# The last head of a chunked Delta net layer: its k and q projected ahead of v and z, one more head's output product inside the output pieces, and the residual added by VectorE

## The chip, the cores and the metric

One NeuronCore of a Trainium2 chip runs the whole program. The metric is the device time of one execution in microseconds (us), the median of several runs. The engines are TensorE (PE; its weight loads are listed as PEld), VectorE (DVE), ScalarE (ACT), GpSimd (POOL) and SyncE (SP), which issues most transfers.

## The reference

Two encoder layers act on 512 tokens of width 1024, each followed by a squared-ReLU MLP. The first mixer is a bidirectional gated Delta net with 8 heads of 128 keys and 128 values, in chunks of 64; the second is a gated linear attention (GLA). Cut to the Delta net and to what surrounds it:

```python
proj = h @ w_in                                  # q, k, v, z of 8 heads, gates
qkv  = silu(depthwise_conv5(proj[..., :3072]))
q, k = l2norm(q) * 128 ** -0.5, l2norm(k)
o    = delta(q, k, v, beta[0], g[0]) + flip(delta(flip(q), flip(k), flip(v), ...))
o    = rmsnorm(o, norm_g) * silu(z)
m    = o @ w_out                                 # (512, 1024) @ (1024, 1024)
x    = layernorm(alpha * x + m)                  # alpha = 4 ** 0.25
x    = layernorm(alpha * x + relu(x @ w1) ** 2 @ w2)
```

## The kernel before, in words

Numbers are float32. A product of two float32 matrices is made of three products of their rounded parts (`mm3`, lines 114 to 116): high by high, high by low, low by high. `split` (lines 95 and 96) makes the parts, the high one by a cast on ACT, the low one by a subtraction on DVE.

The Delta net layer (`gdn`) runs over its heads in a staggered loop of 10 steps. Step i traces the recurrence of head i-2 (`recur`), the solve of head i-1 (`solve`, the inverse of the chunk's triangular matrix), the projections of head i (`project`) and its row factors (`rows`), and at the end `finish` of head i-2, which norms, gates and splits that head's output into its high and low parts. Below, solve(7) means the solve of head 7, which is the last one. In steps 8 and 9 no head is left to project; there the output pieces run, `out_pieces`: the product of heads 0 to 5 with one half (512 columns) of w_out in each step, whose result is added to alpha times x (line 252) and kept in the tiles z.

The order in which an engine gets its instructions is fixed before the run by a planner. It goes by its own estimate of times, and takes among the instructions whose inputs and buffers are then at hand the one traced first. So what is traced later (projections, output pieces) stands between the small steps of what is traced earlier (recurrence, solve). Each engine then takes its instructions strictly in that order, and waits where an input is late.

The names that the steps touch:

- `project` (line 1264 is the SiLU): for one head four projections, in the order k, q, v, z, 24 matmuls each into a PSUM bank with the tag "pj" (three banks). k, q and v go through a convolution of five taps (line 1230 on ACT, line 1234 on DVE). For head 0 SiLU of k and q is called as soon as q is there; for the other heads one call after z does all four. Each call is followed by a load of the table set for exp and ln (line 55).
- `rows`: transposes k and q (PSUM tag "tp", one bank), sums their squares on ACT (line 1286), and ends in the row factors rt (line 1309).
- `solve`: needs rt in `ep` (line 1342), which takes both PSUM banks of the tag "ac"; the same banks are used by all its steps. It ends with xf (line 1483).
- `recur`: lines 1511 to 1536, four steps in both directions; it ends with the output product op (line 1544).
- `finish`: squares (line 1556), scaling (1562), transposes (1566), gate (1572, tile p), and the two parts oh (1573) and ol (1576).
- `out_last`: the product of heads 6 and 7 with both halves of w_out, for four tiles of 128 tokens, followed by LayerNorm of each tile and its transposition for the MLP (lines 159 to 163). In the Delta net it starts each PSUM bank with a float32 product of z with the identity (line 271), and LayerNorm reads the banks. In the GLA layer it is called with `in_ps=False`: there the residual is added by DVE (line 277), which leaves the row sums, and the squares are summed on ACT (line 204).
- `layernorm`: mean and variance by `bn_stats` (lines 208, 209), or from given sums (lines 202 to 205); then lines 211 to 219.

The weights of out_last go into buffers of their own (`homes`): those of the first half into the pair "oah"/"oal", those of the second into two of the four tiles "ol", which hold the low parts of heads 0 to 7, two heads to a tile.

## Time and profile before

| what | value |
|---|---|
| time, median of 3 runs | 1383.04 us (1381.99 to 1383.33) |
| profiled execution, span from the first to the last instruction | 1383.4 us |
| mean granted TensorE clock | 0.996 |
| head 7: last projection done, end of `finish` | 341.6 us, 420.4 us |
| first matmul of the MLP behind it | 435.0 us |

The profiled execution has no time of its own beside its span; the span lies 0.4 us above the median of the runs. In the rows of the profile a line such as `L1342 PE MATMUL ep<-rt,sel` names the line of the program, the engine, the operation, and the tiles written and read. In a timeline the first two numbers are the start and the duration in us, and what stands in square brackets is the idle time before and what ended it. In grouped rows the number after x is a count, then come the sum in us and the mean in ns. Matmuls overlap, so a duration of 0.39 us does not mean that one starts every 0.39 us; 0.23 us is the distance between two starts of the form 128x512.

### The profile page before, as it was taken

To read this page: it belongs to the slowest core of one execution; us is meant where nothing else is said; L and a number is where in the kernel's file an instruction comes from. 1 tells how busy PE (TensorE), PEld (TensorE's weight loads), DVE (VectorE), ACT (ScalarE), POOL (GpSimd) and SP (SyncE) were. 2 spreads that over 40 slices of the span, in tenths; PEclk is the share of its full clock that TensorE was granted. 3 is DMA by queue.
4 is the path that set the end of the run, shared out by engine and by line. 5 is a ranking of instruction groups with operands and counts; after the bars stand their busy time and mean duration, and the time that the engine had idled before them with its cause. 6 is when DMAs were issued, how large, how long until landed. Compare 5 with 4: busy or idle time off the path is not lost.

```text
span 1383.4 us, 21226 instructions
## 1 busy us (share of the span) xinstructions
PE 1353.9 (98%) x8361; PEld 1130.9 (82%) x8361; DVE 1073.9 (78%) x1682; ACT 736.6 (53%) x1438; POOL 71.8 (5%) x111
## 2 busy tenths in 40 slices
PE   9999999999999999999999999999999999999997
PEld 8777787777777888888887888888878888888876
DVE  6687787778677997887957587866879787979665
ACT  4676568665743655555543354654446455546440
POOL 4000000000003600000000000000000000000000
PEclk9999999999999999999999999999999999999999
DMA  6221112211251523253132322221225153431141
GB/s 177 74 62 47 46 32 62 52 42 32 79 154 56 172 77 109 74 153 92 47 112 75 96 89 62 61 62 61 87 66 177 52 152 92 122 88 50 46 151 47
DMA packets 146122, 117.11 MB, mean 85 GB/s; under 512 B 7632, under 2 KB 122440, under 8 KB 146024
## 3 DMA queue, kind: packets, MB, share of 16 engines
q1 hardware_dynamic: 144679, 111.57, 27.4%
q0 software_dynamic: 1344, 4.20, 1.1%
q8 instruction: 65, 1.06, 0.3%
q14 instruction: 34, 0.27, 0.1%
HBM read 113.66 MB, written 2.10 MB: 84 GB/s over the span
## 4 chain that ended last, share of the span: by engine, by line
PE 86%; ACT 6%; DVE 5%; DMA 2%; issue 1%; POOL 0%; DVEq 0%; ACTq 0%; POOLq 0%
PE pj L115 5%; PE pj L116 5%; PE pj L114 5%; PE pjv L114 3%; PE pjv L115 3%; PE pX L114 3%; PE pjv L116 3%; PE pX L115 3%; PE pX L116 3%; PE scp L851 2%; PE fxz L114 2%; PE op L1544 2%; PE fxz L115 2%; PE fxz L116 2%; DMA wst<-in_mlp_w 2%; PE pl L115 2%
## 5 line engine op out<-in xcount | busy, mean ns | idle before, releaser
L95 ACT CAST wh<-wst 128x1024 fp32r<-128x1024 f32 x146 | 152.9, 1050 | 221.6 <-PE pj L115 50.7
L96 DVE TENSOR_TENSOR wl<-wst,wh 128x1024 fp32r<-128x1024 f32 x146 | 177.8, 1225 | 73.3 <-ACT wh L95 73.1
L115 PE MATMUL pj<-xtl,wh 128*128 128x512 f32 (+1 forms) x352 | 127.9, 363 | 0.5 <-DVE xtl L163 0.5
L114 PE MATMUL pj<-xth,wh 128*128 128x512 f32 (+1 forms) x352 | 127.4, 363 | 0.8 <-ACT xth L162 0.7
L116 PE MATMUL pj<-xth,wl 128*128 128x512 f32 (+1 forms) x352 | 127.4, 362 | 0.0
L96 DVE TENSOR_TENSOR w2l<-w2r,w2h 128x1024 fp32r<-128x1024 f32 x84 | 102.5, 1223 | 26.3 <-ACT w2h L95 26.3
L95 ACT CAST w2h<-w2r 128x1024 fp32r<-128x1024 f32 x84 | 88.2, 1050 | 63.5 <-PE pX L116 28.1
L115 PEld LDWEIGHTS pj<-xtl,wh 128*128 128x128 f32 x352 | 67.2, 191 | 10.9 <-DVE xtl L163 0.8
L114 PEld LDWEIGHTS pj<-xth,wh 128*128 128x128 f32 x352 | 66.9, 191 | 11.2 <-ACT xth L162 1.2
L116 PEld LDWEIGHTS pj<-xth,wl 128*128 128x128 f32 x352 | 67.1, 191 | 10.2
L115 PE MATMUL pX<-w2l,ah 128*128 128x512 f32 x192 | 75.0, 391 | 0.0
L116 PE MATMUL pX<-w2h,al 128*128 128x512 f32 x192 | 74.9, 390 | 0.0
L114 PE MATMUL pX<-w2h,ah 128*128 128x512 f32 x192 | 74.8, 393 | 0.0
L95 ACT CAST ah<-h 128x1024 fp32r<-128x1024 f32 x46 | 48.4, 1053 | 47.1 <-PE pX L115 19.3
L336 DVE TENSOR_TENSOR w2r<-w2r 128x1024 f32<-128x1024 f32 x48 | 57.5, 1222 | 0.3
L96 DVE TENSOR_TENSOR al<-h,ah 128x1024 fp32r<-128x1024 f32 x46 | 56.3, 1223 | 0.6
L114 PE MATMUL pjv<-wh,xth 128*128 128x512 f32 x128 | 54.8, 428 | 0.0
L116 PE MATMUL pjv<-wh,xtl 128*128 128x512 f32 x128 | 50.2, 392 | 0.0
L115 PE MATMUL pjv<-wl,xth 128*128 128x512 f32 x128 | 50.0, 390 | 0.0
L116 PEld LDWEIGHTS pX<-w2h,al 128*128 128x128 f32 x192 | 36.1, 188 | 7.5
L116 PE MATMUL pjk<-xth,wl 128*128 128x512 f32 (+1 forms) x112 | 41.8, 373 | 0.0
L114 PE MATMUL pjk<-xth,wh 128*128 128x512 f32 (+1 forms) x112 | 41.7, 372 | 0.0
(477 smaller groups left out, 3932.0 us busy)
## 6 DMA issues: line engine op xcount, KB each, us to landing
wst<-in_mlp_w SPq DMA_DIRECT2D x80, 512.0 KB, 4.4
w2r<-in_mlp_w SPq DMA_DIRECT2D x48, 512.0 KB, 3.8
wst<-in_a_w_in SPq DMA_DIRECT2D x32, 512.0 KB, 4.1
wst<-in_b_w_in SPq DMA_DIRECT2D x32, 256.0 KB, 3.0
wst<-in_a_w_out SPq DMA_DIRECT2D x8, 512.0 KB, 3.7
wst<-in_b_w_in SPq DMA_DIRECT2D x8, 512.0 KB, 3.8
wst<-in_b_w_out SPq DMA_DIRECT2D x8, 512.0 KB, 3.5
xt<-in_x SPq DMA_DIRECT2D x4, 512.0 KB, 5.3
```

The costliest lines, as they stand in the source:

```text
L95: nc.scalar.copy(hi, src)
L96: nc.vector.tensor_tensor(lo, src, hi.bitcast(F32), ALU.subtract)
L114: mm(ps, ah, bh, start=start, stop=False, **kw)
L115: mm(ps, ah, bl, start=False, stop=False, **kw)
L116: mm(ps, al, bh, start=False, stop=stop, **kw)
L336: V.tensor_tensor(blocks[a + (q,)], blocks[a + (q,)], blocks[b + (q,)], ALU.add)
L851: T.matmul(ps[:, n, :], kh[:, sl], qh[:, sl], start=True, stop=True)
L1544: T.matmul(op[:, n, :], l, r, start=i == 0, stop=i == len(mm) - 1)
```

## The change

Three things are changed, nearly all at the end of the Delta net layer.

1. The last head projects like head 0: SiLU of k and q is called after q, and `rows` is traced after q, ahead of v and z. v and z get a SiLU call of their own after z. Head 0, which has the two calls already, now gets the new place of `rows` as well; since its `project` yields once and not eight times for k, the sixteen steps reach into v, and `rows` is traced after 21 of the 24 products of v.
2. The output pieces of the second half take in head 6 as well. The block of weights of heads 6 and 7 for that half is loaded there, into "oah"/"oal", and kept (`held`) for out_last, which then has heads 6 and 7 to do in the first half and head 7 alone in the second. The weights of the first half go into the tiles "ol".
3. The option `in_ps` goes away: the Delta net's out_last adds the residual on DVE with row sums, as the GLA layer does already.

```diff
-    def out_pieces(self, w, ks, lhs, z, tag, halves=(0, 1), piece=2):
+    def out_pieces(self, w, ks, lhs, z, tag, halves=(0, 1), piece=2, keep=None):
         for hf in halves:
-            ws = [self.wrows(w, k * P, hf * 512) for k in ks[::2]]
+            ws = [self.wrows(w, k * P, hf * 512, keep[1] if keep and k + 2 > ks[-1] else None) for k in ks[::2]]
+            if keep:
+                keep[0][hf] = {ks[::2][-1]: ws[-1]}
...
-    def out_last(self, w, ks, lhs, z, tags, par, homes=None, xtags=("tp",), ahead=None, in_ps=True):
+    def out_last(self, w, ks, lhs, z, tags, par, homes=None, xtags=("tp",), ahead=None, held=()):
...
-        ws = [{k: self.wrows(w, k * P, hf * 512, next(homes, None)) for k in ks[hf][::2]} for hf in range(2)]
+        ws = [held[hf] if hf in held else {k: self.wrows(w, k * P, hf * 512, next(homes, None)) for k in ks[hf][::2]}
+              for hf in range(2)]
...
-            if in_ps:
-                nc.tensor.matmul(ps, self.ident, z[t][hf], start=True, stop=False)
             for i, k in enumerate(ks[hf]):
                 ah, al = lhs(k, sl)
-                wh, wl = ws[hf][k - i % 2]
-                self.mm3(ps, ah, al, wh[:, i % 2, :], wl[:, i % 2, :], not in_ps and i == 0, i == len(ks[hf]) - 1)
-            if not in_ps:
-                nc.vector.scalar_tensor_tensor(z[t][hf], ps, 1.0, z[t][hf], ALU.mult, ALU.add, accum_out=sums[t][:, hf:hf + 1])
+                wh, wl = ws[hf][k - k % 2]
+                self.mm3(ps, ah, al, wh[:, k % 2, :], wl[:, k % 2, :], i == 0, i == len(ks[hf]) - 1)
+            nc.vector.scalar_tensor_tensor(z[t][hf], ps, 1.0, z[t][hf], ALU.mult, ALU.add, accum_out=sums[t][:, hf:hf + 1])
             if hf:
                 banks, last = [pss[t, 0], pss[t, 1]], t == NT - 1
-                if in_ps:
-                    self.layernorm(banks, self.xh(t), par, last)
-                else:
-                    self.layernorm(z[t], self.xh(t), par, last, None if last else (sums[t], banks))
+                self.layernorm(z[t], self.xh(t), par, last, None if last else (sums[t], banks))
...
             if new:
-                run(new.project(done), new.rows(done))
-            if i >= A_H:
-                load_z(i - A_H)
-                run(c.out_pieces(w_out, early, lhs, z, "pj", (i - A_H,), 1))
+                work = new.project(done)
+                if new.first_kq:
+                    for _ in range(2 * KT):
+                        next(work)
+                    run(new.rows(done))
+                    run(work)
+                else:
+                    run(work, new.rows(done))
+            if i == A_H:
+                load_z(0)
+                run(c.out_pieces(w_out, early, lhs, z, "pj", (0,), 1))
+            if i == A_H + 1:
+                load_z(1)
+                run(c.out_pieces(w_out, early + [6], lhs, z, "pj", (1,), 1, (held, (pool, "oah", "oal", 1))))
...
-        c.out_last(w_out, [[6, 7]] * 2, lhs, z, ("pj", "ac"), par,
-                   [(pool, "oah", "oal", 1), (pool, "ol", "ol", NT)], ahead=lambda: c.take_ahead(w_next, 3))
+        c.out_last(w_out, [[6, 7], [7]], lhs, z, ("pj", "ac"), par, [(pool, "ol", "ol", NT)],
+                   ahead=lambda: c.take_ahead(w_next, 3), held=held)
...
+        self.first_kq = h in (0, A_H - 1)
...
-            if i == 1 and h == 0:
+            if i == 1 and self.first_kq:
                 c.exp_ln_after(A.activation(kq, kq, AF.Silu))
                 done.add(("kq", h))
             elif i == 3:
-                v = sil[:, 2 if h == 0 else 0:4, :]
+                v = sil[:, 2 if self.first_kq else 0:4, :]
```

More of the change, by code (lines that the diff above doesn't have):

```diff
@@ L254, in out_pieces @@
                         yield 0.68 * piece, 0.0
-    def out_last(self, w, ks, lhs, z, tags, par, homes=None, xtags=("tp",), ahead=None, in_ps=True):
+    def out_last(self, w, ks, lhs, z, tags, par, homes=None, xtags=("tp",), ahead=None, held=()):
         nc = self.nc
         homes = iter(homes or ())
-        ws = [{k: self.wrows(w, k * P, hf * 512, next(homes, None)) for k in ks[hf][::2]} for hf in range(2)]
+        ws = [held[hf] if hf in held else {k: self.wrows(w, k * P, hf * 512, next(homes, None)) for k in ks[hf][::2]}
+              for hf in range(2)]
         if ahead:
             ahead()
-        sums = [None if in_ps else self.small.tile([P, 2], F32, name="lns", tag="lns") for t in range(NT)]
+        sums = [self.small.tile([P, 2], F32, name="lns", tag="lns") for t in range(NT)]
         pss = {}
@@ L742, in gla @@
                    [(pool, "oah", "oal", 1), (pool, "v", "sr", 2), (pool, "F", "F", 2), (pool, "v", "sr", 2)],
-                   ahead=lambda: c.take_ahead(w_next, 3), in_ps=False)
+                   ahead=lambda: c.take_ahead(w_next, 3))
 class GlaHead:
@@ L1183, in run @@
                     pass
-        done = set()
+        done, held = set(), {}
         for i in range(A_H + 2):
```

## The prediction

> **What bounds the kernel now.** I read the page first, for the engine that could be the limit, then the busy time in four stretches around the change, then the engines' timelines along the last head, and last the chain of waits.
>
> ```profile
> span 1383.4 us, 21226 instructions
> PE 1353.9 (98%) x8361; PEld 1130.9 (82%) x8361; DVE 1073.9 (78%) x1682; ACT 736.6 (53%) x1438; POOL 71.8 (5%) x111
> PE 86%; ACT 6%; DVE 5%; DMA 2%; issue 1%; POOL 0%; DVEq 0%; ACTq 0%; POOLq 0%
> ```
>
> TensorE is busy nearly everywhere and carries 86% of the chain. The change touches the end of the Delta net layer, and its first head. Here are four stretches of it: from the start of solve(0) to the last projection (pjz) of head 7, from there to the end of that head's `finish`, on to the first matmul of the MLP, and the first 5 us of the MLP. The columns after the length are busy us of PE, PEld, DVE, ACT and POOL, then the granted clock.
>
> ```profile
> 60.00:341.60 281.60, 276.78 (x2413) 219.35 (x2414) 222.13 (x461) 187.41 (x531) 0.00 (x0) 1.00 0.18 48
> 341.60:420.40 78.80, 78.03 (x625) 60.70 (x624) 54.54 (x116) 48.66 (x147) 2.37 (x4) 1.00 0.36 108
> 420.40:435.00 14.60, 12.74 (x54) 8.42 (x52) 13.97 (x32) 4.59 (x11) 2.99 (x2) 1.00 0.00 1
> 435.00:440.00 5.00, 4.64 (x25) 4.47 (x26) 4.86 (x15) 1.48 (x4) 1.57 (x1) 0.66 0.02 3
> ```
>
> In the second stretch PE is full, but with what? Only a chain of small steps must be done: head 7's rows, solve, recurrence, finish. The rest, the output pieces (oa), stands between them because it is at hand. In the third DVE is full (13.97 of 14.60) and PE is not: LayerNorm sets the pace there. In the fourth the clock has fallen to 0.66.
>
> [...]
>
> Now head 7's chain, by line and start, first on ACT, then DVE, then PE:
>
> ```profile
> 341.57 1.05 ACT L95 CAST wh<-wst 128x1024 fp32r<-128x1024 f32 x1 [6.41 <-PE pjz L115]
> 343.12 1.28 ACT L1264 ACT_TABLE_LOAD   x1
> 344.41 1.92 ACT L1264 ACTIVATE sil<-sil 128x2048 f32<-128x2048 f32 x1
> 346.36 1.07 ACT L1432 CAST pz<-lv 32x128 f16<-32x128 f32 x4
> 347.45 1.28 ACT L55 ACT_TABLE_LOAD   x1
> 358.59 0.57 ACT L1309 COPY rt<-rtp 6x512 bf16<-6x512 bf16 x1
> ```
>
> ```profile
> 337.07 0.74 DVE L1234 SCALAR_TENSOR_TENSOR sil<-pjq,cw,sil 128x510 f32<-128x510 f32 x1
> 355.38 1.33 DVE L1483 SCALAR_TENSOR_TENSOR xf<-Xd,nw 128x512 f32<-128x512 f16 x2
> 397.36 1.47 DVE L1483 SCALAR_TENSOR_TENSOR xf<-Xd,nw 128x512 f32<-128x512 f16 x2
> 419.61 0.82 DVE L1576 TENSOR_TENSOR ol<-p,oh 128x256 fp32r<-128x256 f32 x2
> ```
>
> ```profile
> 361.55 0.60 PE L1342 MATMUL ep<-rt,sel 6*128 6x512 bf16 x2
> 398.39 0.38 PE L1519 MATMUL m<-vt,xf 128*128 128x128 f32 x2
> 407.87 0.39 PE L116 MATMUL oa<-wh,ol 128*128 128x512 f32 x1
> 435.04 0.51 PE L114 MATMUL pj<-xth,wh 128*128 128x256 f32 x2 [0.67 <-ACT xth L162]
> ```
>
> Head 7's q is convolved by 337.8 (337.07 + 0.74), but its SiLU waits for z until 344.4. So `rows` ends with the copy of rt at 359.2, and the first step of solve(7) that needs it, ep, starts at 361.55. Solve(6) had given its last result (xf) at 356.7. From ep on everything is a chain: 36.8 us to the first recurrence product (398.39), 22.0 more to the end of finish (ol, 420.4), 14.6 more to the MLP (435.04).
>
> **The change part by part.**
>
> *k and q first.* Nothing leaves PE: two projections of 24 products move behind `rows`, and the 8 transposes and 4 row products of `rows` move ahead of them. What is added on ACT is one more SiLU call and two more table loads.
>
> ```profile
> L1264 ACT ACTIVATE sil<-sil x8: 1060/1920/1923, 48.6 to 344.4; 128x2048 f32<-128x2048 f32 x7, 128x1024 f32<-128x1024 f32 x1
> ```
>
> Head 0 already does it this way, so the form is in the trace: 1.06 us for 1024 columns. Two such calls instead of one of 1.92 add 0.2 us, and two loads of 1.28 add 2.6: 2.8 us of ACT. Where? The kq call becomes ready at 337.8, inside the 6.41 us in which ACT stood idle (335.2 to 341.57). Load, SiLU and load are 3.6 us and fit there; if that cover is gone they stand ahead of solve(6)'s casts on ACT and cost up to 3.6. The second call falls where the one of 1.92 fell and is 0.9 shorter. What ACT queues behind the new SiLU is solve(6)'s casts of pz, Dd and Xd; PE waits for those.
>
> The Trainium skill, "ScalarE: Activation LUTs", section What ACT_TABLE_LOAD costs, puts a change of table at some 2.66 us with a drain behind the load. By it the two more would cost 5.3. The trace disagrees: load at 343.12, SiLU at 344.41, 1.29 later.
>
> `rows` is then done some 5 us early (16.1 us lie between L1264's load at 343.12 and the end of rt at 359.2; from 337.8 that gives about 354). But solve(7) cannot use all of it. ep needs both PSUM banks of the tag "ac", and solve(6) gives the last one back with xf at 356.7. So ep moves from 361.55 to about 356.8: **4.8 us earlier**. Below: 0, if the planned order leaves ep where it is. Above: 5.7, if solve(6) too ends earlier, by the 0.9 of the shorter SiLU ahead of its casts (L1432). I take 4.8; the 36.8 + 22.0 us behind it keep their length, since PE's filling is the same kind of matmul as before.
>
> *Head 0 as well.* It too now has `rows` traced earlier: `project` of head 0 yields only once for k, so the sixteen steps reach 21 of the 24 products of v, and `rows` comes ahead of the last three and of z.
>
> ```profile
> 47.34 1.28 ACT L1264 ACT_TABLE_LOAD   x1
> 59.98 0.57 ACT L1309 COPY rt<-rtp 6x512 bf16<-6x512 bf16 x1 [2.53 <-PE rtp L1307]
> ```
>
> The SiLU of v and z with its two loads (47.34 to 51.0, 3.7 us) stands among the squares of `rows`; those may now go first, and rt end up to 3.7 earlier. From there to head 7 PE has projections to fill every gap (first row of the stretches, 276.78 of 281.60 busy), so I take 0. The planner deals all that follows anew, though: 1.5 either way, for the places of the identity products and of single waits move with it.
>
> *No identity products.* Eight fp32 products of z with the identity go, each two instructions. The chain of waits names three of them:
>
> ```profile
> 408.26 0.86 PE ob L271 x2
> 417.65 0.86 PE ob L271 x2
> 419.31 0.86 PE ob L271 x2
> 420.17 0.23 PE ob L114
> ```
>
> All eight are 8 x 0.86 = 6.9 us of PE, which is not what they are worth. Three stand ahead of a step of head 7: a recurrence product, the last transpose of finish, the first product with head 7. Something else at hand will take each place, a product of 0.23 at least, and the third was half covered by the wait for ol. So 2 x 0.63 plus 0.3: **1.5 us**. The five others lie where PE waits anyway. Ends: 0 and 6.9.
>
> *Residual by VectorE with sums.* The second layer's output (layer GLA) already works in this way, so each new operation has a row. First DVE and its statistics in this layer, then DVE and ACT in the other one (count | total us, mean ns):
>
> ```profile
> L208 DVE BATCH_NORM_STATS2 bst<-ob 128x6 f32<-128x512 f32 x8 | 5.5, 685 | 0.5 <-PE ob L116 0.5
> ```
>
> ```profile
> L277 DVE SCALAR_TENSOR_TENSOR xt<-ob,xt 128x512 f32<-128x512 f32 x8 | 5.5, 689 | 1.8 <-PE ob L116 1.7
> L208 DVE BATCH_NORM_STATS2 bst<-xt 128x6 f32<-128x512 f32 x2 | 1.4, 688 | 0.0
> L277 DVE DVE_READ_ACCUMULATOR xt<-ob,xt 128x1 f32 x8 | 0.7, 83 | 0.0
> L202 DVE SCALAR_TENSOR_TENSOR bmv<-lns,bias 128x1 f32<-128x1 f32 x3 | 0.7, 220 | 0.1
> L205 DVE SCALAR_TENSOR_TENSOR bmv<-lnq,bias 128x1 f32<-128x1 f32 x3 | 0.6, 214 | 0.0
> ```
>
> ```profile
> L204 ACT ACTIVATE ob<-xt,bmv 128x512 f32<-128x512 f32 x6 | 4.1, 682 | 6.2 <-DVE bmv L202 6.2
> L204 ACT ACTIVATION_READ_ACCUMULATOR ob<-xt,bmv 128x1 f32 x6 | 1.1, 188 | 0.0
> ```
>
> DVE loses six statistics (4.1) and three of four aggregations (0.6) and gains 5.5 + 0.7 + 0.7 + 0.6: 2.8 us more over four tiles. The MLP needs tiles 0 and 1 to start, and their share is 4 x 0.77 + 2 x 0.43 - 4 x 0.69 - 2 x 0.2 = 0.8. ACT gains 5.2, with room. How long it takes from the first half tile on DVE to tile 1's first transposed half on ACT can be read in both layers:
>
> ```profile
> 420.91 2.11 DVE L208 BATCH_NORM_STATS2 bst<-ob 128x6 f32<-128x512 f32 x3 [0.48 <-PE ob L116]
> ```
>
> ```profile
> 434.41 0.59 ACT L162 CAST xth<-tp 128x512 fp32r<-128x512 f32 x1 [1.16 <-PE tp L159]
> ```
>
> ```profile
> 1016.39 0.69 DVE L277 SCALAR_TENSOR_TENSOR xt<-ob,xt 128x512 f32<-128x512 f32 x1 [0.72 <-PE ob L116]
> ```
>
> ```profile
> 1030.05 0.59 ACT L162 CAST xth<-tp 128x512 fp32r<-128x512 f32 x1 [1.45 <-PE tp L159]
> ```
>
> 13.5 us here, 13.7 there, where the products came more slowly. I take **0.5 us later**, between 0.2 and 0.8.
>
> *Head 6 inside the pieces.* Twelve products of head 6 (second half) move from out_last ahead of head 7's end: 12 x 0.23 = 2.8 us of filling for places that identity products held. No DMA is added; one weight block (512 KB) is issued with the pieces instead of after them, on the same SP queue. What is new is a wait: the first half's weights for heads 6 and 7 went into a free pair of buffers, and now go into those of the low parts of heads 0 to 3, which the last output piece still reads. That piece ended at 408.3; with twelve more products, and less PE work elsewhere, I expect 411 to 413. Behind it the split needs 1.05 on ACT (L95) and some 1.2 on DVE. If it ends after head 7 does (420.4 - 4.8 - 1.5 = 414.1), tile 0 is late by up to 2.3; else 0. I take **0.5 later**.
>
> Sum: -4.8 - 1.5 + 0.5 + 0.5 = -5.3. The profiled span is 1383.4, the median of the runs 1383.04, so the execution is an ordinary one: 1383.04 - 5.3 = **1377.7 us**. The MLP behind it only shifts.
>
> **The rivals.**
>
> *PE is the limit after all.* Then all 6.9 us of identity products count, and the idle of the third stretch (14.60 - 12.74 = 1.9) is filled by the earlier chain: 1383.04 - 8.8 = 1374.2. For it: 78.03 of 78.80 busy. Against: the chain behind `ol` is DVE's.
>
> *The chain does not start earlier.* ep stays at 361.5, because the planned order, buffers or the two loads hold it. What is left is -1.5 + 0.5: 1382.0. For it: the order of each engine is fixed before the run, and ACT waited 6.41 us on a full ring while work lay ready.
>
> *The LayerNorm tail gets longer and colder: slower.* Variance now comes by two squares on ACT in series, 2 x (0.68 + 0.19) = 1.7 us per tile, instead of one aggregation of 0.2: 1.5 later, and 0.8 on DVE, 2.3 together. PE, without identity products, idles through it, and the half clock after it is paid twice: at 0.66 the 5 us row loses 5 x 0.34 = 1.7. That makes 4.0 later, 1387.0 if the products were hidden and ep stays. It decides as soon as the chain gains less than 4 us. For it: DVE is full there. Against: 13.5 and 13.7 us above.
> The Trainium skill, "TensorE: Matmul & The Clock Gate", section What's actually happening, has the clock halved after an idle window of about 3.4 us and restored after a busy one. The trace agrees as far as it goes: 0.66 in the row from 435.
>
> **How the numbers follow.** My forecast has 58%, its own range 1374.5 to 1380.2 (first part between 3 and 5.7, identity products between 1 and 3, the tail between 0.2 and 0.8, the weights up to 0.7). PE as limit 12%, no earlier chain 17%, longer tail 13%. About 0.2% (2.8 us) is what a measurement of this kernel can tell from no change. Faster: 58 + 12 = 70%; same: 17%; slower: 13%. The range of 8 in 10 runs from 1373.0, which takes in PE as limit, to 1384.5, which takes in the chain that stays; left out are the cold tail and the far ends.
>
> **What would show it.** Right: a SiLU of 1024 columns on ACT about 338 to 342; `rt` copied before 356; ep of head 7 within 1 us of solve(6)'s last xf; `ol` of head 7 at 413 to 416; the MLP's first product at 429 to 431. Wrong: ep still near 361; ACT's casts of solve(6) later than 346.4 (L1432 starts there now); tile 0's first product waiting for its weights; over 14.5 us from the first residual sum to tile 1's transposed half; a clock under 1.0 for more than 5 us.

## The result, and the profile after

| | before | after |
|---|---|---|
| median of 4 runs | 1383.18 us | 1396.09 us (1395.56 to 1397.82) |
| ratio after to before | | 1.0091, 95% interval 1.0078 to 1.0105 |
| span of the profiled execution, mean granted clock | 1383.4 us, 0.996 | 1393.7 us, 0.988 |

The change made the kernel 0.9% slower, where the prediction had it 0.4% faster. First the page of the changed kernel:

```profile
span 1393.7 us, 21232 instructions
PE 1357.4 (97%) x8345; PEld 1133.7 (81%) x8345; DVE 1080.3 (78%) x1695; ACT 744.6 (53%) x1454; POOL 73.1 (5%) x111
PE 83%; ACT 7%; DVE 7%; DMA 2%; issue 1%; POOL 0%; DVEq 0%; ACTq 0%; POOLq 0%
```

The 16 instructions less on PE are the identity products. PE's busy time nevertheless rose by 3.5 us, though 6.9 us of products went, and its share of the chain fell from 86% to 83%: products ran at a lower clock, and PE waited more. Where, the busy time in five stretches shows (columns as in the prediction: length, busy PE, PEld, DVE, ACT, POOL, then the granted clock): the start of solve(0); the stretch to head 7's last projection; from there to the end of its `finish`; on to the MLP; and the MLP's first 5 us.

```profile
66.00:81.00 15.00, 11.46 (x126) 8.55 (x126) 13.18 (x19) 4.96 (x12) 0.00 (x0) 0.66 0.19 42
341.60:348.60 7.00, 7.00 (x67) 5.52 (x66) 6.95 (x11) 6.28 (x15) 0.00 (x0) 1.00 0.22 77
348.60:426.80 78.20, 77.69 (x649) 61.91 (x649) 53.64 (x116) 45.15 (x138) 2.37 (x4) 1.00 0.27 86
426.80:445.12 18.32, 9.51 (x34) 6.39 (x33) 17.41 (x46) 9.18 (x24) 3.44 (x2) 0.74 0.24 70
445.12:450.12 5.00, 5.00 (x26) 4.93 (x27) 4.93 (x11) 1.60 (x4) 1.57 (x1) 0.59 0.00 0
```

The first stretch in the kernel before:

```profile
66.00:81.00 15.00, 14.89 (x134) 11.20 (x133) 12.19 (x22) 12.60 (x20) 0.00 (x0) 1.00 0.28 71
```

Two places lose. At 66 to 81 us PE is busy 11.46 us in place of 14.89, and at a clock of 0.66: 3.4 us more of idle, and 11.46 x 0.34 = 3.9 us of slower products, an estimate from the mean clock of the row. Together they are near the 7.0 us by which head 7's last projection comes later (348.35; 341.37 before). The other place is the LayerNorm stretch: 18.32 us where it was 14.60, PE idle for half of it, clock 0.74.

Head 7's chain, on ACT, DVE and PE of the changed kernel (its line numbers are up to 10 higher; L1268 is the SiLU, L1317 the copy of rt, L1491 xf, L1350 ep):

```profile
342.28 1.28 ACT L1268 ACT_TABLE_LOAD   x1 [4.65 <-DVE sil L1242]
343.57 1.06 ACT L1268 ACTIVATE sil<-sil 128x1024 f32<-128x1024 f32 x1
361.37 0.56 ACT L1317 COPY rt<-rtp 6x512 bf16<-6x512 bf16 x1
```

```profile
363.70 1.33 DVE L1491 SCALAR_TENSOR_TENSOR xf<-Xd,nw 128x512 f32<-128x512 f16 x2
```

```profile
364.91 0.39 PE L1350 MATMUL ep<-rt,sel 6*128 6x512 bf16 x1
365.66 0.38 PE L1350 MATMUL ep<-rt,sel 6*128 6x512 bf16 x1
```

ep does now come within 1 us of solve(6)'s xf, bank by bank, as forecast; but all of it is 3.4 us later than before, not 4.8 earlier. Against the last projection the chain has gained: from there to solve(7)'s xf are 53.9 us (402.24 - 348.35), before 56.0. The tail gives it back. DVE from finish(7) on:

```profile
422.38 1.23 DVE L96 TENSOR_TENSOR wl<-wst,wh 128x1024 fp32r<-128x1024 f32 x1 [0.53 <-ACT wh L95]
...
424.12 0.87 DVE L1580 SCALAR_TENSOR_TENSOR p<-otp,ng,sil 128x256 f32<-128x256 f32 x2
424.91 1.21 DVE L96 TENSOR_TENSOR wl<-wst,wh 128x1024 fp32r<-128x1024 f32 x1
426.05 0.75 DVE L1584 TENSOR_TENSOR ol<-p,oh 128x256 fp32r<-128x256 f32 x2
427.21 1.23 DVE L96 TENSOR_TENSOR wl<-wst,wh 128x1024 fp32r<-128x1024 f32 x1 [0.42 <-ACT wh L95]
428.36 0.68 DVE L277 SCALAR_TENSOR_TENSOR z<-ob,z 128x512 f32<-128x512 f32 x1
```

Weight splits (L96) stand before p, between p and ol, and before the first residual sum; the kernel before had none between 413.1 and 435. The MLP starts at 445.12 in place of 435.04: +10.1, of which 7.0 are from the first place.

### The profile page after: what moved, and what is told of

Read it like the earlier page. It is cut to its first block, busy times and chain, and to the rows that moved or that the text cites. A ratio compares the mean times of both kernels' runs of the same rounds, so it can differ in the third digit from the quotient of the medians.

```text
span 1393.7 us, 21232 instructions
## 1 busy us (share of the span) xinstructions
PE 1357.4 (97%) x8345; PEld 1133.7 (81%) x8345; DVE 1080.3 (78%) x1695; ACT 744.6 (53%) x1454; POOL 73.1 (5%) x111
## 4 chain that ended last, share of the span: by engine, by line
PE 83%; ACT 7%; DVE 7%; DMA 2%; issue 1%; POOL 0%; DVEq 0%; ACTq 0%; POOLq 0%
PE pj L114 5%; PE pj L115 5%; PE pj L116 5%; PE pjv L115 3%; PE pjv L114 3%; PE pjv L116 3%; PE pX L114 3%; PE pX L115 3%; PE pX L116 3%; PE scp L848 2%; PE fxz L114 2%; DMA wst<-in_mlp_w 2%; PE fxz L115 2%; PE fxz L116 2%; PE pl L115 2%; PE pl L116 2%
## 5 line engine op out<-in xcount | busy, mean ns | idle before, releaser
L96 DVE TENSOR_TENSOR wl<-wst,wh 128x1024 fp32r<-128x1024 f32 x146 | 178.2, 1225 | 72.0 <-ACT wh L95 71.7
L96 DVE TENSOR_TENSOR w2l<-w2r,w2h 128x1024 fp32r<-128x1024 f32 x84 | 102.8, 1226 | 26.7 <-ACT w2h L95 26.7
L116 PEld LDWEIGHTS pj<-xth,wl 128*128 128x128 f32 x352 | 67.0, 190 | 10.2
L96 DVE TENSOR_TENSOR al<-h,ah 128x1024 fp32r<-128x1024 f32 x46 | 56.2, 1221 | 0.6
```

The costliest lines, as they stand in the source:

```text
L96: nc.vector.tensor_tensor(lo, src, hi.bitcast(F32), ALU.subtract)
L116: mm(ps, al, bh, start=False, stop=stop, **kw)
```

## The experiments

The change has four parts: **A**, head 0's rows early; **B**, the last head first with k and q; **C**, head 6 in the pieces; **D**, the residual by VectorE without identity products. Fifteen runs took them apart. The time is the ratio to the kernel before with its interval. "z end" is the start of head 7's last projection product, and the last column the us from there to the MLP's first product, which leaves out what came earlier. It leaves out what comes later too: from the MLP's first product to the end these traces take 945.0 (e1) to 950.3 us (e2), so the time and the last column of a row can differ by some us. Runs stand beside different executions of the kernel before (1383.2 to 1384.2), so a difference in time between two runs of different groups (after, e1 to e4, e5 to e8, e9 to e12, e13 to e15) is taken from their ratios.

| run | what it is | median us | ratio (95%) | z end | z end to MLP |
|---|---|---|---|---|---|
| before | | 1383.2 to 1384.2 | 1 | 341.37 | 93.67 |
| after | A+B+C+D | 1396.09 | 1.0091 (1.0078 to 1.0105) | 348.35 | 96.77 |
| e1 | B+C+D | 1389.07 | 1.0042 (1.0030 to 1.0054) | 341.84 | 97.96 |
| e2 | A | 1394.02 | 1.0074 (1.0061 to 1.0088) | 348.42 | 95.51 |
| e3 | B | 1384.64 | 1.0010 (1.0001 to 1.0019) | 341.31 | 93.85 |
| e4 | D | 1386.65 | 1.0017 (1.0008 to 1.0026) | 341.02 | 96.86 |
| e5 | B, traced otherwise | 1382.37 | 0.9990 (0.9982 to 0.9999) | 340.65 | 91.55 |
| e6 | D, tile 2 by bn_stats | 1386.00 | 1.0017 (1.0007 to 1.0026) | 341.64 | 94.65 |
| e7 | D, no GpSimd addition | 1384.88 | 1.0009 (1.0000 to 1.0018) | 342.40 | 94.84 |
| e8 | e1, other weight buffers | 1389.22 | 1.0041 (1.0027 to 1.0055) | 341.69 | 97.26 |
| e9 | A, projections first | 1388.64 | 1.0039 (1.0025 to 1.0052) | 345.00 | 93.77 |
| e10 | e5, no GpSimd addition | 1380.90 | 0.9977 (0.9967 to 0.9988) | 342.00 | 90.72 |
| e11 | e10, a split later | 1380.80 | 0.9979 (0.9969 to 0.9988) | 340.67 | 90.82 |
| e12 | e8, two splits later | 1387.34 | 1.0020 (1.0012 to 1.0029) | 341.69 | 96.04 |
| e13 | e11 with D | 1382.55 | 0.9988 (0.9979 to 0.9997) | 342.09 | 91.79 |
| e14 | e13, no squares | 1383.57 | 0.9998 (0.9988 to 1.0008) | 343.02 | 92.41 |
| e15 | before, no GpSimd addition | 1382.40 | 0.9988 (0.9978 to 0.9997) | 341.72 | 92.74 |

The theory at the start: A loses about 7 us early, which reach the end; B gains 2 to 3; the rest is lost in the tail.

### e1 and e2: is it head 0?

e1 undoes A, e2 makes it alone:

```diff
 # e1, against after
-                if new.first_kq:
+                if new.first_kq and i:
 # e2, against before
-                run(new.project(done), new.rows(done))
+                work = new.project(done)
+                if i == 0:
+                    for _ in range(2 * KT):
+                        next(work)
+                    run(new.rows(done))
+                    run(work)
+                else:
+                    run(work, new.rows(done))
```

> The changed kernel with one part undone: head 0's rows and solve are again built behind its v and z. The last head first with k and q, head 6 in the pieces and the residual by VectorE stay. Theory T (the early solve of head 0 starves TensorE between 66 and 81 us and halves its clock, and the 7.0 us by which head 7's last projection ends later reach the end): 1396.1 - 7 = 1389, 1387 to 1391; the profile has the last projection of head 7 at 341 to 342 us and a clock of 1.00 from 60 to 100 us. Rival R1 (those 7 us vanish before the end, because the chain from solve(6) sets it; all of the loss is made in the tail): 1396, within 1.5. Both have the LayerNorm tail as in the changed kernel: 15 to 17 us from the first residual sum to tile 1's transposed half.

> The kernel before with one part of the change alone: head 0's rows and solve come out ahead of its v and z. Nothing else is touched. Theory T: 1383.2 + 7 = 1390, 1388 to 1392, with head 7's last projection at 347 to 349 us and the half clock between 66 and 81 us. Rival R1 (slack ahead of the end of the chain absorbs it): 1383, within 1.5.

Without A the change costs 0.42% and not 0.91%; A alone costs 0.74%, 10.2 us of 1384, which is above theory T's 5 to 9. The early loss is not absorbed: R1 falls. Here are 60 to 80 us, first in the kernel before, then in e2:

```profile
60.00:80.00 20.00, 19.89 (x149) 14.88 (x150) 15.25 (x26) 15.67 (x29) 0.00 (x0) 1.00 0.28 74
60.00:80.00 20.00, 16.44 (x173) 12.23 (x171) 19.08 (x32) 8.46 (x16) 0.00 (x0) 0.83 0.09 25
```

DVE is now the full engine. Why PE starves, e2 shows on PE, DVE and ACT:

```profile
67.96 0.40 PE L115 MATMUL pjz<-xtl,wh 128*128 128x512 f32 x1
...
77.32 0.77 PE L116 MATMUL pjz<-xth,wl 128*128 128x512 f32 x1
```

```profile
75.55 1.21 DVE L96 TENSOR_TENSOR wl<-wst,wh 128x1024 fp32r<-128x1024 f32 x1
```

```profile
62.30 2.06 ACT L95 CAST wh<-wst 128x1024 fp32r<-128x1024 f32 x2
```

Head 1's z has its first two products, and the third needs the low part of the weights. Their high part was made by 63.4 (the first of the two casts). But the split stands on DVE until 75.55, behind solve(0)'s steps and head 1's convolutions, which now meet. (The expectation of e9 below names a later cast, at 69.7; that one belongs to a projection after it.) For 9 us PE has only solve(0)'s small products, with waits of 0.5 to 0.8 us between them, and two others. That "PE has projections to fill every gap" was true of the average, not of this place.

### e9: the same, with solve(0) behind head 1's projections

```diff
+            if i == 1:
+                run(new.project(done))
             if mid:
                 run(mid.solve(done))
...
```

> Head 0's rows and solve early, as in e2_head0_only, but head 1's projections are traced ahead of solve(0), so that its convolutions and weight splits go before solve(0)'s steps. In e2 TensorE had no projection to run from 68.2 to 77.3 us but for two products: the split of the next weights stood on VectorE until 75.55, behind solve(0)'s steps and convolutions, though its high part was there at 69.7; the clock fell to half. Theory T (the loss is this starvation, made by solve(0)'s precedence on VectorE): PE over 19.5 of 20 us and a clock of 1.00 from 60 to 80 us, head 7's last projection back at 341 to 343, and 1384 to 1386 in place of 1394. Rival L (the loss is in what else comes with the early rows: two table loads among the squares and another order of all that follows): 1390 or more.

Two stretches of e9:

```profile
60.00:80.00 20.00, 20.00 (x110) 15.48 (x108) 14.57 (x22) 14.21 (x25) 0.00 (x0) 1.00 0.39 101
140.00:160.00 20.00, 18.34 (x126) 13.98 (x125) 18.19 (x38) 9.95 (x32) 0.00 (x0) 1.00 0.00 1
```

The hole and the half clock of 60 to 80 are gone, and with them 3.4 of 7.0 us at z end and 0.35% of the time, 4.8 us. So the starvation is a cause, and about half of A's cost. The rest lies between the two theories: 3.6 us at z end stay, 1.7 of them a new hole at 140 to 160 (before: 20.00 busy). By what step of the order it comes is left open, and so is why A costs 10.2 alone and 6.8 (0.49%) within the change; by the intervals the first is known to some 2 us and the second to some 2.5.

### e3 and e5: the last head's chain

e3 makes the new order for the last head alone. e5 also changes where it is traced: solve(6) up to its last steps, then k, q and rows of head 7, then the rest of solve(6), then v and z.

```diff
 # e5, against e3
+            inv = mid.solve(done) if mid else iter(())
+            if i == A_H - 1:
+                for step in inv:
+                    if step[0] == "op":
+                        break
...
                     run(new.rows(done))
+                    run(inv)
                     run(work)
```

> The kernel before with one part of the change alone: the last head's k and q, and its rows and solve, come ahead of its v and z. Theory T (the chain gains what the changed kernel's chain gained on its last projection, 2 to 3 us, bounded by solve(6)'s last copies out of the shared banks): 1380.5, 1379 to 1382, with the last tile copies of solve(7) at 393 to 396 us where the kernel before has 398. Rival R3 (the tail ahead of the LayerNorm is bound by TensorE's remaining output products, not by the chain, so an earlier chain ends nothing earlier): 1383, within 1. The prediction's own sum for this part, 4.8 us: 1378.4.

> The last head first with k and q, as in e3_last_kq_only, but head 7's k, q and rows are now traced ahead of the last steps of solve(6) (qk, qke, xf), so that VectorE's row factors (rw and the rest) no longer stand behind solve(6)'s xf in its queue. In e3 rw ran at 357.16 though lnr was there at 354.0, so rt (359.15) and ep (361.2) came where the kernel before has them. Theory Q (that queue place is what kept ep): ep moves to 357 to 358.5. Then two cases for the time. The prediction's working (from ep on it is a chain of fixed length): 3 to 4 us earlier at the MLP and 1381 to 1382 against the 1384.6 of e3. Rival P (TensorE is full from 341.6 to 420.4, 77.86 of 78.80 in e3, so an earlier chain only lets other products come later): at most 1 us earlier, 1383.5 to 1385.

e3 gains nothing. Its ACT, DVE and PE say why:

```profile
338.74 1.06 ACT L1267 ACTIVATE sil<-sil 128x1024 f32<-128x1024 f32 x1
344.02 1.06 ACT L1271 ACTIVATE sil<-sil 128x1024 f32<-128x1024 f32 x1
345.09 1.07 ACT L1439 CAST pz<-lv 32x128 f16<-32x128 f32 x4
353.66 0.31 ACT L1296 ACTIVATE lnr<-ssp,bias 128x8 f32<-128x8 f32 x1
359.15 0.56 ACT L1316 COPY rt<-rtp 6x512 bf16<-6x512 bf16 x1
```

```profile
356.56 0.69 DVE L1490 SCALAR_TENSOR_TENSOR xf<-Xd,nw 128x512 f32<-128x512 f16 x1 [0.18 <-PE nw L1489]
357.16 0.17 DVE L1303 SCALAR_TENSOR_TENSOR rw<-lnr,gc 128x8 f32<-128x8 f32 x1
```

```profile
361.19 0.38 PE L1349 MATMUL ep<-rt,sel 6*128 6x512 bf16 x1
```

The SiLU comes at 338.74, where the prediction put it. lnr is there at 354.0. But rw, the first of the row factors, stands behind solve(6)'s xf on DVE and starts at 357.16, so rt and ep are where they were. And solve(6)'s casts (L1439) still wait for the other SiLU. Now e5, the same rows:

```profile
341.14 1.08 ACT L1445 CAST pz<-lv 32x128 f16<-32x128 f32 x4
...
350.03 1.06 ACT L1277 ACTIVATE sil<-sil 128x1024 f32<-128x1024 f32 x1
```

```profile
351.64 1.46 DVE L1496 SCALAR_TENSOR_TENSOR xf<-Xd,nw 128x512 f32<-128x512 f16 x2
...
353.44 0.17 DVE L1309 SCALAR_TENSOR_TENSOR rw<-lnr,gc 128x8 f32<-128x8 f32 x1 [0.34 <-ACT lnr L1302]
```

```profile
355.44 0.56 ACT L1322 COPY rt<-rtp 6x512 bf16<-6x512 bf16 x1
```

```profile
356.75 0.60 PE L1355 MATMUL ep<-rt,sel 6*128 6x512 bf16 x2
```

ep comes at 356.75; the prediction had 356.8. The agreement is luck: the prediction had rt done about 354 and ep held by the banks until xf ends at 356.7, while in e5 xf ends at 353.1 and rt, done at 356.0, is the later of the two. Nor did it come by the route that my expectation gave: rw still runs behind xf, but xf no longer holds it, since rw waits 0.34 us for lnr after that. What moved is the second SiLU (v and z) with its two loads, from 344.02 to 350.03, behind solve(6)'s casts, which start 4 us earlier and pull xf with them; lnr, too, is there 0.6 us earlier (353.4). Both effects changed in one run and were not separated.

Did the earlier chain pay? Against z end, ep is 3.8 us earlier than in e3, the MLP 2.3, and the time is 0.20% less, 2.8 us. So neither the fixed length behind ep (3 to 4) nor a full PE (at most 1): a good half of it arrives.

### e4, e6 and e7: the residual

e4 is D alone, `in_ps=False` in the call of the kernel before. e6 and e7 are edits to it, of which e15 and e10 make the second in kernels with the identity products:

```diff
 # e6: tile 2 by bn_stats
-self.layernorm(z[t], self.xh(t), par, last, None if last else (sums[t], banks))
+self.layernorm(z[t], self.xh(t), par, last, None if last or (t == 2 and len(tags) == 2) else (sums[t], banks))
 # e7: second halves by VectorE alone
+self.layernorm(z[t], self.xh(t), par, last or len(tags) == 2, None if last else (sums[t], banks))
```

> The kernel before with one part of the change alone: the Delta net's last output product adds its residual by VectorE with sums into SBUF, and the identity products are gone; head 6 is still in the last product. Theory T (the sums queue on VectorE behind the next weights' splits, the squares of the variance hold the banks of the later tiles, and TensorE falls to half clock through the LayerNorms): 3 to 5 us slower, 1386 to 1388, 15 to 17 us from the first sum to tile 1's transposed half. Rival R2 (the tail's loss comes from head 6 in the pieces: fewer products are left in the last product to cover the LayerNorms, and its weights wait for head 7's output buffers; the sums themselves cost what the prediction said): the identity products' 1.5 gained and 0.5 lost, 1382, within 1.5.

> The residual by VectorE, as in e4_residual_only, but tile 2 (of 0 to 3) takes its variance by bn_stats on VectorE and not by squares on ScalarE. In e4 ScalarE stood 1.89 us (429.1 to 430.97) before tile 2's square, which waited for its mean (L202 at 430.73), and tile 0's transposed half, ready at about 430.4, was cast only at 431.69 behind it. Theory S (the squares of the later tile block ScalarE ahead of the casts): MLP start 1.3 to 2 us earlier than e4's 437.88, time 1384.5 to 1385.5. Rival V (VectorE is the limit, and two statistics more, 1.4 us, stand there instead): as e4 or up to 1 later, 1386.5 to 1388.

> The residual by VectorE, as in e4_residual_only, but the second halves of these four LayerNorms are scaled and shifted by one VectorE operation each (0.74 us) and not by ScalarE (0.72) and an addition on GpSimd (1.6 to 1.8). In e4 a VectorE operation of 0.15 or 0.21 us took 1.22 (L174 at 429.58) and 1.16 (L205 at 433.61), both ending with the GpSimd addition that ran then. Theory G (VectorE is held by GpSimd's additions, twice 1.0 us ahead of the MLP, and tile 1's second half waits for the addition): those two last 0.15 to 0.2, and the MLP starts 1.5 to 2.5 us earlier than in e4: 1384 to 1385. Rival V (VectorE is the limit and gets 0.74 a tile more): within 0.7 of e4's 1386.6.

D alone costs 0.17%, 2.4 us: theory T against R2. The end of finish is 1.05 us earlier (ol 418.56, before 419.61), near the 1.5 that the identity products were to give. From there on it loses: from the first DVE operation of the LayerNorm to the MLP are 17.6 us (420.27 to 437.88), before 14.1. DVE, POOL and ACT of e4:

```profile
429.58 1.22 DVE L174 SCALAR_TENSOR_TENSOR rst<-bmv,rst 128x1 f32<-128x1 f32 x1
430.73 0.21 DVE L202 SCALAR_TENSOR_TENSOR bmv<-lns,bias 128x1 f32<-128x1 f32 x1
```

```profile
429.17 1.62 POOL L219 TENSOR_TENSOR xt<-xt,lnp 128x512 f32<-128x512 f32 x1 [29.84 <-ACT xt L218]
```

```profile
430.97 0.69 ACT L204 ACTIVATE ob<-z,bmv 128x512 f32<-128x512 f32 x1 [1.89 <-DVE bmv L202]
...
431.69 0.56 ACT L162 CAST xth<-tp 128x512 fp32r<-128x512 f32 x1
```

Read them as a chain: GpSimd adds from 429.17 to 430.79; a DVE operation that elsewhere takes 0.15 ends at 430.80; behind it tile 2's mean (L202); ACT waits 1.89 us for that mean with tile 2's square; and behind the square stands the cast of tile 0's transposes, which the MLP needs. e6 takes the square away: the MLP 2.2 us earlier against z end, but the same ratio of the time, 1.0017; on the time it is undecided. e7 takes the addition away: 2.0 us against z end, 0.08% of the time (1.1 us), with intervals that lie on each other. In its trace the two operations that G names take 0.15 and 0.21 us (L174 at 431.78, L205 at 435.97), so the hold is gone, as G says. But e7 also makes these second halves shorter, 0.74 us on DVE in place of 0.73 on ACT and 1.62 on GpSimd, and which of the two brings the MLP forward was not separated. D then costs 0.09% and is still no gain.

### e8 and e12: head 6 in the pieces

e1, against e3 and e4 together, leaves 2.0 us for C (0.42 - 0.10 - 0.17 = 0.15% of 1384); the three intervals together are wider than that, and from z end to the MLP the same difference is 0.9 us. In e1 the scaled output fo of finish(7) came at 419.33, before 416.30. DVE there (L173 and L180 belong to finish):

```profile
414.93 1.23 DVE L96 TENSOR_TENSOR wl<-wst,wh 128x1024 fp32r<-128x1024 f32 x1
...
417.41 1.23 DVE L96 TENSOR_TENSOR wl<-wst,wh 128x1024 fp32r<-128x1024 f32 x1 [0.58 <-ACT wh L95]
418.55 0.15 DVE L173 TENSOR_TENSOR rst<-rsy 128x4 f32<-128x4 f32 x1
```

e8 gives the first half's weights buffers of their own; e12 also queues two of the next layer's splits behind the small steps of finish (`marks` are its last exp on ACT and ors on DVE):

```diff
 # e8, against e1
-        c.out_last(w_out, [[6, 7], [7]], lhs, z, ("pj", "ac"), par, [(pool, "ol", "ol", NT)],
...
+        held[0] = {6: (owh, Pair(owl))}
+        c.out_last(w_out, [[6, 7], [7]], lhs, z, ("pj", "ac"), par, None,
 # e12, against e8
+        def ahead():
+            c.take_ahead(w_next, 1)
+            with tc.issue_after(heads[-1].marks[0].ins), tc.issue_after(heads[-1].marks[1].ins):
+                c.ahead += [c.wcols(w_next, f * P) for f in range(1, 3)]
...
```

> As e1_no_head0 (the change without its part for head 0), but the weights of heads 6 and 7 for the first half of the last product go into buffers of their own, not into the low-part tiles that the last output piece still reads. The low part is subtracted in two operations of 512 columns. In e1 those splits came late (ScalarE 408.49 and 413.86, VectorE 413.67, 414.93 and 417.41, some of them the next layer's weights behind it), between the small steps of head 7's finish, and the scaled output fo came at 419.33 where the kernel before has 416.30. Theory W (the late home pushes the splits into the finish): fo at 416 to 417, MLP start 2 to 3 us earlier than e1's 439.80, time 1386 to 1387. Rival C (the loss comes from head 6's products inside the pieces, which stand ahead of the finish's transposes on TensorE): as e1, 1389, within 1.

> As e8_own_weight_home (the change without its part for head 0, first half's weights in buffers of their own), but two of the next layer's weight splits are queued behind the small steps of head 7's finish, as in e11. In e8 they still stood there (ScalarE 413.69 and 414.88, VectorE 414.76 and 416.57), because the ring buffers they go into come free only with the last output piece, which ends some 7 us later than before; fo came at 418.49. Theory W' (head 6 in the pieces costs by pushing these splits into the finish): fo at 416 to 416.7, MLP start 1.5 to 2.2 us earlier than e8's 438.95, time 1387 to 1387.7 against 1389.2. Rival C (the products of the pieces on TensorE are the cost): fo no earlier than 418.

e8 changes nothing in the time: the weights' home is not the cost, and my theory W falls. e12, on DVE and ACT:

```profile
416.49 0.15 DVE L180 TENSOR_TENSOR ors<-rsv,rst 128x4 f32<-128x4 f32 x1
416.56 2.35 DVE L96 TENSOR_TENSOR wl<-wst,wh 128x1024 fp32r<-128x1024 f32 x2
```

```profile
417.16 1.13 ACT L1588 ACTIVATE fo<-op,ors 128x128 f32<-128x128 f32 x4
```

fo is 1.3 us earlier than in e8 (417.16 against 418.49), short of the 416 to 416.7 of theory W' and earlier than the 418 of rival C. The time is 0.21% less, 2.9 us, just beyond what the two intervals leave open, and within 0.4 us of e4's. So as far as C has a cost, most of it is that the next layer's splits stand among the small steps of finish. That they come late because the last output piece ends some 7 us later (its last product starts at 415.3 in e1, 407.9 before) and frees the weight ring later is argued from these times and was not tried alone; nor was the late queueing tried on D without C.

### e10, e11 and e15: can it be faster?

```diff
 # e10 against e5, e15 against before
-                    self.layernorm(banks, self.xh(t), par, last)
+                    self.layernorm(banks, self.xh(t), par, True)
```

e11 queues the third split as e12 does.

> As e5_rows_before_xf (identity products and bn_stats of the kernel before are kept, last head first with k and q, its rows ahead of solve(6)'s xf), with the second halves of the four LayerNorms done by VectorE alone, without GpSimd's addition. Theory G (in the kernel before, too, a VectorE operation of 0.15 us is held by that addition: L174 took 1.25 at 427.93, and tile 1's second half waits 1.3 to 1.7 for the addition): MLP start 1.0 to 2.0 earlier than in e5 (432.20), time 1381 against 1382.4. Rival V (VectorE is full in this stretch, 13.97 of 14.60, so 0.74 more a tile gives it back): as e5, 1382 to 1383.

> As e10, but the third of the next layer's weight splits is queued behind the small steps of head 7's finish (on ScalarE behind its last exp, on VectorE behind ors), where VectorE then waits 2.4 us for the transposes. In e5 that split stood in the middle of them (ScalarE 411.51, VectorE 412.59), and from the last op to fo were 5.3 us where the kernel before has 3.6. Theory W (splits among the small steps of finish cost their own length on the chain): fo 1.2 to 1.7 earlier than in e10, and 1 to 1.5 us less time. Rival P (TensorE is full and the products behind come no earlier): within 0.5 of e10.

> The kernel before with one edit: the second halves of the four LayerNorms in the Delta net are scaled and shifted by VectorE, without GpSimd's addition. Theory G (the hold by GpSimd costs by itself): 1 to 1.5 us less than the kernel before, 1382.5 to 1383; with the 1.7 of e5 that makes e10's 3. Rival (it pays only where the chain is early): 1384, within 0.5.

e15 gains 0.12%, e5 0.10%, e10 0.23%: they add up, and e10 beats both kernels. At the MLP, against z end, e10 is 0.8 us earlier than e5, where theory G had 1.0 to 2.0. Its LayerNorm stretch:

```profile
420.40:432.70 12.30, 12.30 (x53) 8.52 (x52) 11.95 (x27) 2.75 (x7) 0.00 (x0) 1.00 0.00 1
```

PE is now full there, at a clock of 1.00. That fits what e11 shows: from the last op to fo are 4.0 us, 1.4 less than in e10, and the MLP comes no earlier against z end. Rival P.

### e13 and e14: does the removal pay once PE is full?

e13 is e11 with `in_ps=False`, squares only for tiles 0 and 1; e14 has no squares at all.

```diff
 # e13, in out_last; e14 leaves out "t == 2 and"
+self.layernorm(z[t], self.xh(t), par, last or len(tags) == 2, None if last or t == 2 and len(tags) == 2 else (sums[t], banks))
```

> As e11 (early chain, no GpSimd addition, third split late), with the residual by VectorE with sums and no identity products; squares on ScalarE for tiles 0 and 1, bn_stats for tiles 2 and 3. Theory P (TensorE is full from 341.6 us to the MLP in e11, so 6.9 us of identity products are now on its path): MLP start 3 to 6 us earlier relative to head 7's last projection, 1375 to 1378. Theory S (the longer statistics, sums, squares and two small operations for each tile, set the tail once more as in e4 and e7): 16 us from the first sum to the MLP where e11 has 14.8, and 1381 to 1383.

> As e13, but the variance of all four tiles comes from bn_stats on VectorE over the summed rows; no squares on ScalarE, so TensorE's banks come free with the sums. Theory S1 (the squares, their place on ScalarE and the banks they hold, are the cost of the sums): faster than e13 by 1 us or more. Theory S2 (VectorE's own work is the cost; four more statistics of 0.69 stand ahead of tiles 0 and 1): slower than e13 by 0.5 to 2 us.

e13 is 0.09% slower than e11 by the ratios (1.2 us), e14 another 1.0 us, and at the MLP, against z end, each is later too (1.0 and 0.6 us). The intervals of neighbours lie on each other, so the losses are not clear of noise; the gains that theories P and S1 promised are not there. So even here the 6.9 us of products bring nothing when they go, and the squares are not what the sums cost. The stretch from 430 to 440 us, and the last product of out_last, in e11:

```profile
430.00:440.00 10.00, 10.00 (x81) 9.53 (x81) 9.27 (x23) 3.79 (x8) 0.78 (x3) 1.00 0.01 2
```

```profile
431.26 0.39 PE L116 MATMUL ob<-ol 128*128 128x512 f32 x1
```

and in e13:

```profile
430.00:440.00 10.00, 7.21 (x34) 6.83 (x35) 8.70 (x20) 2.65 (x7) 0.00 (x0) 0.52 0.00 0
```

```profile
425.68 0.40 PE L116 MATMUL ob<-ol 128*128 128x512 f32 x1
```

In e13 PE has little to do ahead of the MLP (at 433.88; it is busy 1.99 of the last 5 us), and the mean clock of the row is 0.52; in e11 it has work throughout and stays at 1.00. The rule of the Trainium skill, "TensorE: Matmul & The Clock Gate", section What's actually happening, that idle windows halve the clock and a busy one restores it, agrees with these two rows. The identity products are only part of the difference. In e13 the last real product of out_last comes 8.2 us ahead of the MLP, in e11 0.2 us. In the other kernels it is the same: without identity products and with the sums that product comes 7.3 to 10.2 us ahead of the MLP, and the clock in the last 5 us is 0.50 to 0.73, in the MLP's first 5 us 0.50 to 0.62. With them it comes 0.2 to 2.3 us ahead, and the clock is 1.00 in both stretches, but for 0.66 behind the MLP's start in the kernel before and in e2. So with the sums the products of the last tiles run early, and PE is left idle behind them. Whether that or the missing identity products lowers the clock was not separated.

## Why the prediction was wrong, point by point

- **Head 0: the step that failed.** "From there to head 7 PE has projections to fill every gap [...] so I take 0", 1.5 either way. It cost 7.0 us at z end (6.5 against e1) and 6.8 of the time (after against e1). The shift itself was also mis-sized: rt of head 0 was to end "up to 3.7 earlier" and came 9.0 earlier (50.96; 59.98 before). The row behind the step was one of 281.6 us. From 60 to 80 us alone DVE was busy 15.25 of 20 in the kernel before, and with solve(0) some 7 us earlier 19.08 (e2; its ep starts at 54.42, before at 61.89). Where DVE carries the steps of a solve, the convolutions and the weight splits at once, PE's filling fails, since each projection needs its split.
- **k and q first: -4.8 was 0 or a small loss in the form that was made** (e3, 0.10% slower). SiLU and lnr came on time; the step "rows is then done about 354" failed, since DVE's queue held rw behind xf. The rival "the planned order leaves ep where it is" had 17% and was right for this part. That an earlier ep pays is borne out by e5, where the mechanism was in part another (rt and not xf is last) and the 356.75 agrees by luck. But "the 36.8 + 22.0 us behind it keep their length" failed: of 3.8 us, 2.3 arrive.
- **Identity products: -1.5** was about right at the end of finish (1.05 in e4), and wrong behind it. "The five others lie where PE waits anyway" counted them as free. Without them, and with the last products early, PE's wait became long enough for the clock to fall (0.50 to 0.73 ahead of the MLP, 1.00 with them); their own share in that is not known.
- **The sums: +0.5 was mis-sized.** From the first DVE operation to the MLP e4 takes 3.5 us more. I compared 13.5 with the 13.7 of the GLA layer and took the length over; here tile 2's square and the held DVE operation fall in front of tile 0's cast (e4), and PE's own work behind the sums ends early. With the gain above, D is +2.4 in place of -1.0.
- **Head 6 in the pieces: +0.5 was 2.0 or less**, and for another reason. I looked for a late first product of tile 0; the late splits instead came between the small steps of finish.
- **The rival that ended on the other side** had the right place (PE idle, half clock ahead of the MLP and behind it). Its squares in series are not borne out by e14, which has none and is no faster, and that its 1387.0, meant for the whole change, is near D alone (1386.65) is luck. It got 13% because the GLA stretch spoke against it, and it lacked head 0 altogether.
- Of the signs set out beforehand, those for right failed (the SiLU at 343.57, rt at 361.37, ol at 426.05, the MLP at 445.12) but for ep within 1 us of xf; of those for wrong, later casts of solve(6) (354.82, against 346.4), the 14.5 us from the first sum to tile 1's transposed half (16.1: 428.36 to 444.48) and the clock under 1.0 for over 5 us came true. The 7.0 us from head 0 are in all these times.
- The upper end of the forecast's own range does not follow from its terms: 3 + 1 - 0.8 - 0.7 = 2.5 us of gain give 1380.5, not 1380.2. It changes nothing.

By the ratios the loss of 12.6 us (0.91%) divides into 6.8 (A, after against e1), 1.4 (B), 2.4 (D) and 2.0 for C. C is what is left, so the sum proves nothing about the parts, and B and C are each near what noise can make.

## What to carry to other kernels

When a step is traced earlier, price it in the stretch into which it moves and on the engine that feeds the matmuls, not by how full TensorE is on average. A chain starts earlier only if each in-order queue on its way lets its small steps pass: look at what stands ahead of the first of them on VectorE and ScalarE. Before products that look like pure overhead are taken out, ask what TensorE will do through a stretch that another engine sets: here its remaining products ran early, it idled, and its clock fell as the next stage began.

## What the runs showed of the hardware

- While GpSimd added one 128x512 tile to another, a VectorE operation of 128x1 that takes 0.15 us elsewhere was held to the addition's end: 427.93 + 1.25 = 429.18 against 427.45 + 1.71 = 429.16 in the kernel before, 430.80 against 430.79 in e4. Without the additions the same line took 0.15 in e10. The Trainium skill, "GPSIMD Engine Reference", section Key points, says that the two share SBUF interfaces; that agrees. Not every operation was held. In the kernel before, a subtraction and a statistic that read PSUM ran beside the second addition (430.87 to 432.14) in their usual 0.68 and 0.69 us (L163 at 430.74, L208 at 431.34). Those held read two operands from SBUF. In e4 that was also LayerNorm's first pass over tile 3, 1.77 us at 440.10, since with the sums it reads z from SBUF; in the kernel before the same pass reads PSUM and took 0.74 at 437.26 beside the third addition. Doing the addition on VectorE gained 0.12% (e15), though VectorE was full there; that is the hold and the shorter path of these halves together.
- The clock fell within a few us of scattered products, not of silence alone: in e2 PE was busy 2.95 of 5 us at 70 to 75 and 4.21 of 5 at 75 to 80, and the mean clock was 0.76 and 0.55. In the changed kernel PE was busy 11.46 of 15 us at 66 to 81, at 0.66.
